# Hymba layer, one core: the MLP's down-projection as seven block products, with its left factors formed in the up-projection, and the first pair of each token half as eight block products

## The chip, the cores and the metric

One core of one Trainium2 chip. The metric is the device time in microseconds (us) of the whole kernel, from a launch on the chip. The kernel before took a median of 3212.68 us in three runs (3212.42 to 3213.5).

Engines: PE is TensorE (matrix products, with weights loaded by PEld), DVE is VectorE, ACT is ScalarE, POOL is GpSimd, SP issues the DMAs of this kernel.

## The reference, cut to what matters

The kernel computes one bidirectional encoder layer on 2048 tokens of width 1024 in float32: attention and a state-space group side by side, an output projection, and a squared-ReLU MLP. The change concerns the last three lines of the layer:

```python
m = rms_norm(h, g_pre_mlp[i]) @ w_mlp_up[i]          # 2048 x 1024 times 1024 x 4096
m = jnp.square(jax.nn.relu(m)) @ w_mlp_down[i]       # 2048 x 4096 times 4096 x 1024
h = h + rms_norm(m, g_post_mlp[i])
```

## The kernel before

**Precision.** Every fp32 factor of a matmul is split in two fp32r parts, h = cast(x) on ACT (line 125) and l = x - h on DVE or POOL (line 126). A product is three matmuls: h·h, h·l, l·h. A matmul is 128x128 by 128x512.

**Order.** The program is written in loops, and a scheduler decides each engine's order of instructions from its own model of their times. On every engine the instructions then run in that order, and an instruction that waits holds back all behind it. DMAs are issued by SP in one such queue.

**Up-projection** (lines 1244 to 1434). It already uses seven block products for eight (Strassen in Winograd's form). The work is cut into 32 pairs: two halves of the tokens (ct, 1024 each), and in each 16 pairs of hidden blocks of 128 columns (NP = 16). For a pair, `up_prep` loads a 1 MB tile of the up weights (`raw`) and forms the seven left factors from its four blocks: a11, a21+a22-a11, a12, a11-a21, a21+a22, a22, a12-a21-a22+a11. I call them f0 to f6. f0, f2 and f5 are plain blocks; f1, f3, f4 and f6 are sums made by POOL in a tile `st` (line 1264: two, one, one and three operations). Each is split into `ah` and `al`. Tiles `raw` and `st` come from the pool `wraw` with two buffers each, `ah` and `al` from `apool` with nine. The seven right factors, B11, T2, B21, T3, T1, T4, B22, are formed from the normed activations once per token half by `t_slice` (lines 1304 to 1321), for each of four slices k of the inner dimension, and stay in SBUF. `up_pair` multiplies, one product after another: 7 x 4 slices x 3 = 84 matmuls; `up_pair_k`, used for pairs 0, 15 and 16, runs over the slices outside, so that it can begin when the first slice is ready. The output sums of Winograd's form are built from PSUM by DVE, and `relu2` (ReLU and square on ACT, lines 1340 and 1341) gives four blocks of the hidden activations per pair, each written to DRAM (`MD`) with 256 KB.

**Down-projection** (lines 1443 to 1543). Plain: eight blocks b of 512 hidden columns, in each block four quarters c of the tokens. For a quarter the left factors (`mraw`, 256 KB each, four of them) are read back and split, for a block the weights (`raw`, four tiles of 512 KB) are loaded and split. `down` does, for each tile of 128 tokens and each half of the outputs, 4 x 3 = 12 matmuls into one PSUM tile (line 1514) and adds it on DVE to the sum `acc` in SBUF (line 1519). So a block and a quarter take 96 matmuls. In the last block `finish` follows each token tile: sum of squares on ACT, gain on DVE, 1/rms on POOL, scale and residual on DVE, output.

Of the kernel before, what the change touches and what calls it, by code (L numbers as in the profile page):

```python
# [51 lines left out]
def hymba_layer_kernel(  # L52
# [53 lines left out]

    HTD = mk(dram, [2, 4, 128, 4, 512], "HTD")
    MD = mk(dram, [2, FF // 128, 128, 1024], "MD")
# [1062 lines left out]
    tst = hw.enter_context(pool("tst", 2))  # L1171
    wraw = hw.enter_context(pool("wraw", 2))
# [17 lines left out]
    def out_tile(t, between):  # L1190
# [12 lines left out]
        V.tensor_copy(s2, p[:, 0:4])  # L1203
# [45 lines left out]
    def up_prep(n):  # L1249
# [6 lines left out]
        for first, *more in ((a11,), (a21, (add, a22), (sub, a11)), (a12,), (a11, (sub, a21)), (a21, (add, a22)),  # L1256
                             (a22,), (a12, (sub, a21), (sub, a22), (add, a11))):
# [23 lines left out]
    for t in range(NT):  # L1281
        last.append((t, out_tile(t, lambda: hn_T(*last.pop(0)) if len(last) == 2 else None)))
        if t in (10, 11):
            s_load(0, t - 10)
        if t >= NT - 7:
            facs.append(next(prep))
# [9 lines left out]
    upr = up_.enter_context(pool("upr", 6, "right"))  # L1296
# [7 lines left out]
    def t_slice(ct, k):  # L1304

        raw = RAW.pop((ct, k))
        b11, b12, b21, b22 = (raw[:, i] for i in range(4))
        l = {n: rt() for n in (T1, T3, T2, T4)}
        split(b11, *TB[B11, k], G)
        G.tensor_tensor(out=l[T1], in0=b12, in1=b11, op=ALU.subtract)  # L1310
        V.tensor_tensor(out=l[T3], in0=b22, in1=b12, op=ALU.subtract)
        V.tensor_tensor(out=l[T2], in0=b22, in1=l[T1], op=ALU.subtract)
        G.tensor_tensor(out=l[T4], in0=l[T2], in1=b21, op=ALU.subtract)
        split(l[T2], *TB[T2, k])
        split(b21, *TB[B21, k])
        split(l[T3], *TB[T3, k])
        split(l[T1], *TB[T1, k])
        split(l[T4], *TB[T4, k])
        split(b22, *TB[B22, k], G)
        if (ct, k + 2) in ((ct, 2), (ct, 3)):  # L1320
            s_load(ct, k + 2)
# [15 lines left out]

    def relu2(c, src, n, odd, half):

        S.activation(out=c, in_=src, func=AF.Relu)  # L1340
        S.activation(out=c, in_=c, func=AF.Square)
        ct, j = n // NP, n % NP
        Y.dma_start(out=MD[ct, 2 * j + odd][:, half * 512:(half + 1) * 512], in_=c)

# [75 lines left out]

    def stepper(n):

        nxt = up_prep(n + 1)

        def step(i):
            facs.append(next(nxt))
        return step

    t_slice(0, 0)
    t_slice(0, 1)  # L1430
    up_pair_k(0, stepper(0), lambda k: t_slice(0, k + 2) if k < 2 else None)
    hn_T(*last.pop(0))
    for n in range(1, NP - 1):
        up_pair(n, stepper(n))
    s_load(1, 0)
    s_load(1, 1)
    up_pair_k(NP - 1, stepper(NP - 1), lambda k: t_slice(1, k))
    up_pair_k(NP, stepper(NP), lambda k: None)
# [5 lines left out]
    FB = 4  # L1444
    NB = FF // 128 // FB
    dps = [ctx.enter_context(pool("dp0", FB))]
    draw = ctx.enter_context(pool("draw", 1))

    def d_load(b):
        for q in range(FB):  # L1450
            fo = (b * FB + q) * 128
            raw = draw.tile([128, D], F32, tag="raw", name="raw")
            Y.dma_start(out=raw, in_=w_mlp_down[0, fo:fo + 128, :])
            dh = dps[b % 2].tile([128, D], F32R, tag="dh", name="dh")
            dl = dps[b % 2].tile([128, D], F32R, tag="dl", name="dl")
            split(raw, dh, dl)
            yield dh, dl

    def m_load(b, c):

        for q in range(FB):
            raw = draw.tile([128, 512], F32, tag="mraw", name="mraw")
# [106 lines left out]
```

## Time and profile before

| what | value |
|---|---|
| median of three runs | 3212.68 us |
| the profiled execution's own time | 3213.55 us |
| its span, first to last instruction | 3211.7 us |
| mean granted TensorE clock | 0.973 |
| PE / DVE / ACT / POOL busy | 94% / 58% / 51% / 39% |
| up-projection's first matmul | 1859.1 us after the span's start |
| last matmul of the down-projection | 3201.9 us |

Busy shares are averages over the whole span; the parts before 1840 us are the attention, the state-space group and the output projection, which the change leaves alone. A row of a group gives busy time, mean length of one in ns, and after the bar the idle time of the engine ahead of them with what ended it. A row of the timeline gives start, length, engine, line and operation, output and inputs, and in brackets the idle time before it and what released it.

### The profile page before, as it was taken

To read this page: it belongs to the slowest core of one execution; us is meant where nothing else is said; L and a number is where in the kernel's file an instruction comes from. 1 tells how busy PE (TensorE), PEld (TensorE's weight loads), DVE (VectorE), ACT (ScalarE), POOL (GpSimd) and SP (SyncE) were. 2 spreads that over 40 slices of the span, in tenths; PEclk is the share of its full clock that TensorE was granted. 3 is DMA by queue.
4 is the path that set the end of the run, shared out by engine and by line. 5 is a ranking of instruction groups with operands and counts; after the bars stand their busy time and mean duration, and the time that the engine had idled before them with its cause. 6 is when DMAs were issued, how large, how long until landed. Compare 5 with 4: busy or idle time off the path is not lost.

```text
span 3211.7 us, 42406 instructions
## 1 busy us (share of the span) xinstructions
PE 3032.7 (94%) x14455; PEld 2419.7 (75%) x14455; DVE 1848.8 (58%) x2893; ACT 1638.6 (51%) x3081; POOL 1255.2 (39%) x2363
## 2 busy tenths in 40 slices
PE   6999988989999999999879879999999999999998
PEld 6899956666777766678767658886888888888887
DVE  6333278767888876675356584448444234444447
ACT  4333356988777799974435445445445421111112
POOL 4222245775888876600032275447544000000002
PEclk8999989999999999999989989999999999999999
DMA  4232231211001022232246543333333422222215
GB/s 151 65 86 74 73 75 27 58 46 33 20 18 27 24 70 85 65 113 63 65 112 179 164 154 115 109 114 119 109 107 106 142 81 73 73 79 73 69 63 203
DMA packets 244377, 279.51 MB, mean 87 GB/s; under 512 B 35920, under 2 KB 180688, under 8 KB 243136
## 3 DMA queue, kind: packets, MB, share of 16 engines
q1 hardware_dynamic: 242112, 275.10, 28.1%
q8 instruction: 113, 1.85, 0.2%
q10 hardware_dynamic: 1792, 1.57, 0.2%
q14 instruction: 104, 0.85, 0.1%
q0 software_dynamic: 256, 0.14, 0.0%
HBM read 181.31 MB, written 95.36 MB: 86 GB/s over the span
## 4 chain that ended last, share of the span: by engine, by line
PE 57%; issue 6%; DVE 4%; ACT 4%; POOL 3%; DMA 2%; SPq 0%; POOLq 0%; DVEq 0%; ACTq 0%
PE dn L1514 20%; PE pE L1329 5%; PE pB L1329 5%; PE pA L1329 4%; PE s L619 3%; PE s L621 2%; PE s L620 2%; PE z L1079 2%; PE X L611 2%; PE pF L1329 2%; PE X L612 2%; PE X L613 2%; PE mxp L573 2%; POOL rs_r L132 1%; DMA rb<-RD 1%
## 5 line engine op out<-in xcount | busy, mean ns | idle before, releaser
L627 DVE TENSOR_TENSOR pl<-s,ph 128x512 fp32r<-128x512 f32 x512 | 350.2, 686 | 163.1 <-ACT s L626 157.0
L623 ACT ACTIVATE ph<-s 128x512 fp32r<-128x512 f32 (+1 forms) x544 | 323.4, 595 | 171.9 <-PE s L621 158.6
L1514 PE MATMUL dn<-dl,ah 128*128 128x512 f32 x1024 | 398.8, 389 | 0.0
L1514 PE MATMUL dn<-dh,ah 128*128 128x512 f32 x1024 | 398.8, 389 | 0.0
L1514 PE MATMUL dn<-dh,al 128*128 128x512 f32 x1024 | 398.7, 390 | 0.0
L574 DVE TENSOR_REDUCE mx<-mxp 128x1 f32<-128x512 f32 x512 | 343.0, 684 | 59.3 <-PE mxp L573 56.2
L125 ACT CAST ah<-mraw 128x512 fp32r<-128x512 f32 x128 | 79.5, 621 | 454.3 <-DMA mraw<-MD 273.8
L626 ACT ACTIVATE s<-s 128x512 f32<-128x512 f32 x512 | 304.1, 594 | 0.7
L1498 POOL TENSOR_TENSOR ss<-s2f 128x1 f32<-128x1 f32 x16 | 11.2, 699 | 702.2 <-ACT jk L1495 702.2
L1264 POOL TENSOR_TENSOR st<-raw 128x512 f32<-128x512 f32 x128 | 173.9, 1359 | 263.6 <-DVE al L126 263.5
L619 PE MATMUL s<-ql,kh 96*128 96x512 f32 (+1 forms) x544 | 226.9, 417 | 15.1 <-ACT ZS L937 4.9
L611 PE MATMUL X<-pl,vt 128*65 128x512 f32 x512 | 209.2, 409 | 29.8 <-DVE pl L627 27.9
L1519 DVE TENSOR_TENSOR acc<-dn,acc 128x512 f32<-128x512 f32 x224 | 153.0, 687 | 133.2 <-PE dn L1514 132.8
L1514 PEld LDWEIGHTS dn<-dl,ah 128*128 128x128 f32 x1024 | 192.4, 188 | 39.8
L1514 PEld LDWEIGHTS dn<-dh,al 128*128 128x128 f32 x1024 | 192.4, 188 | 39.7
L1514 PEld LDWEIGHTS dn<-dh,ah 128*128 128x128 f32 x1024 | 192.3, 188 | 39.7
L620 PE MATMUL s<-qh,kl 96*128 96x512 f32 (+1 forms) x544 | 218.3, 401 | 0.0
L621 PE MATMUL s<-qh,kh 97*128 97x512 f32 (+1 forms) x544 | 215.0, 401 | 0.7 <-DMA qh<-nm 0.7
L573 PE MATMUL mxp<-kh,qh 96*128 96x512 f32 x512 | 199.3, 411 | 13.2 <-DVE mx L574 5.2
L612 PE MATMUL X<-ph,vt 128*64 128x512 f32 x512 | 205.3, 401 | 0.0
L613 PE MATMUL X<-ph,vt 128*65 128x512 f32 x512 | 205.1, 401 | 0.0
L126 DVE TENSOR_TENSOR al<-mraw,ah 128x512 fp32r<-128x512 f32 x128 | 88.5, 691 | 197.8 <-ACT ah L125 188.2
(811 smaller groups left out, 7822.8 us busy)
## 6 DMA issues: line engine op xcount, KB each, us to landing
raw<-in_w_mlp_up_dram SPq DMA_DIRECT2D x32, 1024.0 KB
MD<-r SPq DMA_DIRECT2D x128, 256.0 KB
mraw<-MD SPq DMA_DIRECT2D x128, 256.0 KB
xt<-in_x_dram SPq DMA_DIRECT2D x32, 512.0 KB
raw<-in_w_mlp_down_dram SPq DMA_DIRECT2D x32, 512.0 KB
ug<-UD SPq DMA_DIRECT2D x32, 256.0 KB
HD<-o SPq DMA_DIRECT2D x16, 512.0 KB
traw<-HTD SPq DMA_DIRECT2D x8, 1024.0 KB
```

What stands on the lines that cost most here:

```text
L574: V.reduce_max(out=mxs[n][:, j, b:b + 1], in_=p, axis=AX.X)
L611: T.matmul(out=X[:65], lhsT=v[:, t, 0:65], rhs=pl_, start=(t == 0), stop=False)
L612: T.matmul(out=X[:64], lhsT=v[:, t, 65:129], rhs=ph_, start=False, stop=False)
L613: T.matmul(out=X[:65], lhsT=v[:, t, 0:65], rhs=ph_, start=False, stop=False)
L619: T.matmul(out=s[:m], lhsT=kh[0:96, cs], rhs=ql, start=True, stop=False)
L620: T.matmul(out=s[:m], lhsT=kl[:, cs], rhs=qh[0:96], start=False, stop=False)
L621: T.matmul(out=s[:m], lhsT=kh[:, cs], rhs=qh, start=False, stop=True)
L623: S.activation(out=ph_[:m], in_=s[:m], func=AF.Exp, scale=SCALE)
L626: S.activation(out=s, in_=s, func=AF.Exp, scale=SCALE)
L627: V.tensor_tensor(out=pl_, in0=s, in1=f(ph_), op=ALU.subtract)
L1329: T.matmul(out=p, lhsT=a[:, k], rhs=b, start=(first and k == 0 and j == 0), stop=(k == 3 and j == 2), skip_group_check=not first)
L1514: T.matmul(out=p, lhsT=a[:, ts_], rhs=c[:, hs], start=(q == 0 and w == 0), stop=(q == FB - 1 and w == 2))
```

## The change

**Down-projection.** The product of hidden activations (token halves x hidden blocks) and weights (hidden blocks x output halves) is taken in Winograd's form too. A unit is a block b of 512 hidden columns (two pairs) and a quarter g of the tokens, in which two sets of 128 tokens are paired with two others. It has seven products of 2 token sets x 2 inner blocks x 3 = 12 matmuls: 84. The left factors (a11, a12, a21, a22, s1 = a21+a22, s2 = s1-a11, s4 = a12-s2, a11-a21) are formed in `relu2` of the up-projection, two on DVE and two on POOL; `MD` keeps seven blocks for each pair, so seven writes of 256 KB instead of four, and the down-projection reads seven tiles per unit. The right factors are formed from the weights by `w_factors`: per block 14 POOL operations (lines 1555), 14 casts and 14 subtractions, spread over the last unit (g = 3) of the block before, into a ring of 16 buffers. The seven results go into `acc` with DVE operations from PSUM (12 per unit) and POOL operations in SBUF (6 per unit, lines 1652, 1661, 1662).

**First pairs.** Pair 0 and pair 16 use eight block products (`up_pair_c`, 96 matmuls): they need only the plain blocks B11, T4's place used for b12, B21 and B22. The T slices are formed later: T1 to T3 from the raw tiles (slices 0 and 1 on POOL), T4 afterwards on POOL from the split parts.

**Buffers.** `wraw` has one buffer instead of two, so one `raw` and one `st`; `tst` 3 instead of 2, `upr` 8 instead of 6. `finish` splits the scaling over DVE, ACT and POOL and takes its two work tiles from the pool `wr` of two buffers.

```diff
-    MD = mk(dram, [2, FF // 128, 128, 1024], "MD")
+    MD = mk(dram, [2, FF // 256, 128, 7, 512], "MD")
...
-    tst = hw.enter_context(pool("tst", 2))
-    wraw = hw.enter_context(pool("wraw", 2))
+    tst = hw.enter_context(pool("tst", 3))
+    wraw = hw.enter_context(pool("wraw", 1))
...
+        for first, *more in ((a11,), (a12,), (a21,), (a22,)) if j == 0 else seven:
...
+    def b_slice(ct, k):
+        raw = RAW[ct, k]
+        for i, n in enumerate((B11, T4, B21, B22)):
+            split(raw[:, i], *TB[n, k])
...
+    def t_slice(ct, k, eng=V):
         raw = RAW.pop((ct, k))
...
+        eng.tensor_tensor(out=t1, in0=b12, in1=b11, op=ALU.subtract)
+        eng.tensor_tensor(out=t3, in0=b22, in1=b12, op=ALU.subtract)
+        eng.tensor_tensor(out=t2, in0=b22, in1=t1, op=ALU.subtract)
...
+        for n, t in ((T2, t2), (T3, t3), (T1, t1)):
+            split(t, *TB[n, k])
+    def t4_slice(k):
+        (th, tl), (bh, bl) = TB[T2, k], TB[B21, k]
+        t = rt()
+        G.tensor_tensor(out=t, in0=f(th), in1=f(tl), op=ALU.add)
+        G.tensor_tensor(out=t, in0=t, in1=f(bh), op=ALU.subtract)
+        G.tensor_tensor(out=t, in0=t, in1=f(bl), op=ALU.subtract)
+        split(t, *TB[T4, k])
...
     def relu2(c, src, n, odd, half):
         S.activation(out=c, in_=src, func=AF.Relu)
         S.activation(out=c, in_=c, func=AF.Square)
...
+        if len(blocks) == 4:
+            a11, a12, a21, a22 = (blocks.pop(x) for x in ((0, 0), (1, 0), (0, 1), (1, 1)))
+            s1, s2, s4 = rt(), rt(), rt()
+            V.tensor_tensor(out=s1, in0=a21, in1=a22, op=ALU.add)
+            put(4, s1)
+            V.tensor_tensor(out=a21, in0=a11, in1=a21, op=ALU.subtract)
+            put(3, a21)
+            G.tensor_tensor(out=s2, in0=s1, in1=a11, op=ALU.subtract)
+            put(1, s2)
+            G.tensor_tensor(out=s4, in0=a12, in1=s2, op=ALU.subtract)
+            put(6, s4)
...
+    def w_factors(b):
...
+        for first, *more in ((b11,), (b22, (sub, b12), (add, b11)), (b21,), (b22, (sub, b12)), (b12, (sub, b11)),
+                             (b22, (sub, b12), (add, b11), (sub, b21)), (b22,)):
+            for fp in range(2):
...
+                    for op, x in more:
+                        G.tensor_tensor(out=st, in0=src, in1=blk(x), op=op)
+                        src = st
+                split(src, h, l)
...
+    def down(b, g, step):
...
+        for i in range(7):
...
+                for fp in range(2):
...
+                    for j, (x, y) in enumerate(((mh, wh), (mh, wl), (ml, wh))):
+                        T.matmul(out=ps, lhsT=x[:, c], rhs=y, start=(first and fp == 0 and j == 0),
+                                 stop=(fp == 1 and j == 2), skip_group_check=not first)
...
+                if i == 0:
+                    S.copy(out=p1, in_=ps)
+                elif i == 1:
+                    V.tensor_tensor(out=u2, in0=ps, in1=p1, op=ALU.add)
+                    if b > 0:
+                        G.tensor_tensor(out=c12, in0=c12, in1=u2, op=ALU.add)
...
+                elif i == 3:
+                    V.tensor_tensor(out=u3, in0=ps, in1=p1, op=ALU.add)
+                    if b > 0:
+                        G.tensor_tensor(out=c22, in0=c22, in1=u3, op=ALU.add)
+                        G.tensor_tensor(out=c21, in0=c21, in1=u3, op=ALU.add)
```

What this makes of the order shows at three places. The first is POOL in the up-projection, before the change; `st<-raw` opens a factor, `st<-st,raw` continues it, and the numbers tell the tiles apart (raw_22420 and raw_22574 belong to two pairs).

```order
L1264 TENSOR_TENSOR st_22548<-raw_22420 128x512
L1264 TENSOR_TENSOR st_22548<-st_22548,raw_22420 128x512
L1264 TENSOR_TENSOR st_22595<-raw_22574 128x512
L1264 TENSOR_TENSOR st_22548<-st_22548,raw_22420 128x512
L1264 TENSOR_TENSOR st_22595<-st_22595,raw_22574 128x512
L1264 TENSOR_TENSOR st_22635<-raw_22574 128x512
L1264 TENSOR_TENSOR st_22658<-raw_22574 128x512
L1264 TENSOR_TENSOR st_22702<-raw_22574 128x512
```

The next pair's f1 stands among the operations of f6. The same place after the change, where L1371 is s2 and L1373 is s4 of the pair whose products run:

```order
L1371 TENSOR_TENSOR r_23099<-r_23098,r_23011 128x512
L1266 TENSOR_TENSOR st_23034<-raw_22973 128x512
L1373 TENSOR_TENSOR r_23100<-r_23073,r_23099 128x512
L1266 TENSOR_TENSOR st_23057<-raw_22973 128x512
L1266 TENSOR_TENSOR st_23111<-raw_22973 128x512
L1266 TENSOR_TENSOR st_23111<-st_23111,raw_22973 128x512 x2
L1266 TENSOR_TENSOR st_23158<-raw_23137 128x512
L1266 TENSOR_TENSOR st_23158<-st_23158,raw_23137 128x512
L1266 TENSOR_TENSOR st_23198<-raw_23137 128x512
L1371 TENSOR_TENSOR r_23263<-r_23262,r_23175 128x512
L1373 TENSOR_TENSOR r_23264<-r_23237,r_23263 128x512
L1266 TENSOR_TENSOR st_23221<-raw_23137 128x512
```

The next pair's f1 now stands behind all of f6; f3 stands between s2 and s4 in one pair and ahead of s2 in the next, and f4 and f6 always behind s4. The second place is SP in the same stretch, after the change: the weight load of a pair among the writes of `MD`.

```order
L1359 DMA MD_81<-r_23098 128x512
L1359 DMA MD_81<-r_23099 128x512
L1359 DMA MD_81<-r_23094 128x512
L1359 DMA MD_81<-r_23100 128x512
L1359 DMA MD_81<-r_23175 128x512
L1254 DMA raw_23137<-in_w_mlp_up_dram 128x8x256
L1359 DMA MD_81<-r_23214 128x512
```

r_23098 to r_23100 are s1, s2, a11-a21 and s4 of one pair, r_23175 is the first block of the next. Before the change the load stood behind a pair's first block in the same way, with no sums in front. The third place is DVE in the down-projection after the change, in a unit g = 3: `al` are left factors, `wl` right factors of the next block, the other rows take results from PSUM.

```order
L127 TENSOR_TENSOR wl_28020<-wst_28021,wh_28019 128x512
L1668 TENSOR_TENSOR acc_26685<-pE_27892,acc_26685 128x512
L127 TENSOR_TENSOR al_28043<-mraw_28040,ah_28042 128x512
L1650 TENSOR_TENSOR u2_27949<-pB_27988,p1_27948 128x512
L1650 TENSOR_TENSOR u2_27952<-pB_27997,p1_27951 128x512
L127 TENSOR_TENSOR wl_28047<-raw_27976,wh_28046 128x512
L127 TENSOR_TENSOR al_28075<-mraw_28072,ah_28074 128x512
L127 TENSOR_TENSOR wl_28051<-raw_27978,wh_28050 128x512
L1657 TENSOR_TENSOR acc_26685<-pA_27954,acc_26685 128x512
L1657 TENSOR_TENSOR acc_26685<-pA_27962,acc_26685 128x512
L127 TENSOR_TENSOR wl_28079<-wst_28080,wh_28078 128x512
L127 TENSOR_TENSOR al_28109<-mraw_28106,ah_28108 128x512
```

Before the change DVE's rows there are additions into `acc` from PSUM and an `al` or `dl` after every second of them; now operations on two SBUF inputs and evictions alternate.

More of the change, by code (lines that the diff above doesn't have):

```diff
@@ L1419, in up_pair_k, with up_pair_c, step, before @@
         slices(3)
+    def up_pair_c(n, before, behind, step):
+        mine = take()
+        outs = []
+        for half, (b1, b2) in enumerate(((B11, B21), (T4, B22))):
+            for odd in range(2):
+                outs.append((pa("c"), odd, half, mine[2 * odd], mine[2 * odd + 1], b1, b2))
+        for k in range(4):
+            before(k)
+            for i, (p, odd, half, a1, a2, b1, b2) in enumerate(outs):
+                for w, (left, b) in enumerate(((a1, b1), (a2, b2))):
+                    ah, al = left
+                    bh, bl = TB[b, k]
+                    for j, (x, y) in enumerate(((ah, bh), (ah, bl), (al, bh))):
+                        T.matmul(out=p, lhsT=x[:, k], rhs=y, start=(k == 0 and w == 0 and j == 0),
+                                 stop=(k == 3 and w == 1 and j == 2))
+                if k == 3:
+                    relu2(rt(), p, n, odd, half)
+                    if i > 0:
+                        step()
+            if k in (1, 2):
+                step()
+            if k == 2:
+                step()
+            behind(k)
+        step()
     def stepper(n):
         nxt = up_prep(n + 1)
-        def step(i):
-            facs.append(next(nxt))
-        return step
[L1429 to L1432, printed above, removed]
+        def step(i=None):
+            w = next(nxt, None)
+            if w is not None:
+                facs.append(w)
+        return step
+    b_slice(0, 0)
+    b_slice(0, 1)
+    t_slice(0, 0, G)
+    b_slice(0, 2)
+    def before(k):
+        if k == 1:
+            hn_T(*last.pop(0))
+            t_slice(0, 1, G)
+        elif k == 2:
+            b_slice(0, 3)
+            t_slice(0, 2)
+        elif k == 3:
+            t_slice(0, 3)
+    up_pair_c(0, before, t4_slice, stepper(0))
     for n in range(1, NP - 1):
         up_pair(n, stepper(n))
[L1435 to L1438, printed above, removed]
+    for k in range(3):
+        s_load(1, k)
+    def behind(k):
+        b_slice(1, k)
+        t_slice(1, k)
+    up_pair_k(NP - 1, stepper(NP - 1), behind)
+    up_pair_c(NP, lambda k: None, t4_slice, stepper(NP))
     for n in range(NP + 1, 2 * NP - 1):
@@ L1441, in hymba_layer_kernel @@
     hw.close()
[L1444 to L1457, printed above, removed]
@@ L1459, in m_load @@
-    def m_load(b, c):
-        for q in range(FB):
-            raw = draw.tile([128, 512], F32, tag="mraw", name="mraw")
-            Y.dma_start(out=raw, in_=MD[c // 2, b * FB + q][:, (c % 2) * 512:(c % 2) * 512 + 512])
-            mh = apool.tile([128, 4, 128], F32R, tag="ah", name="ah").rearrange("p k c -> p (k c)")
-            ml = apool.tile([128, 4, 128], F32R, tag="al", name="al").rearrange("p k c -> p (k c)")
-            split(raw, mh, ml)
-            yield mh, ml
-    ds, ms = [], []
@@ L1499, in finish @@
         r = rstd_of(st, D)
[L1500 removed]
+        for half, eng in ((0, V), (1, G)):
             hs = slice(half * 512, (half + 1) * 512)
[L1502 to L1519 removed]
@@ new lines, in hymba_layer_kernel, with step @@
+    parts = [(b, g) for b in range(NB) for g in range(4)]
+    for _ in nm:
+        pass
+    for n, (b, g) in enumerate(parts):
+        nm = m_factors(*parts[n + 1]) if n + 1 < len(parts) else iter(())
+        if g == 3:
+            nwf = w_factors(b + 1) if b + 1 < NB else iter(())
+        def step(i, behind):
+            if behind:
+                next(nm, None)
+                if g == 3:
+                    next(nwf, None)
+                    next(nwf, None)
+            elif n == 0:
+                while len(WF) <= i:
+                    next(nwf, None)
+        down(b, g, step)
+        if g == 3:
+            for _ in nwf:
+                pass
+            del WF[:7]
```

181 lines of the change are left out of this document (112 added, 69 removed).

## The prediction

> **What bounds the kernel now.** I read the page's busy times first, then the chain of waits, then the table by stretches for the two stages that the change rewrites.
>
> ```profile
> PE 3032.7 (94%) x14455; PEld 2419.7 (75%) x14455; DVE 1848.8 (58%) x2893; ACT 1638.6 (51%) x3081; POOL 1255.2 (39%) x2363
> 2508.86 625.62 PE dn L1514 x2761
> L1514 PE MATMUL dn<-dl,ah 128*128 128x512 f32 x1024 | 398.8, 389 | 0.0
> 2260.00:2320.00 60.00, 60.00 (x266) 49.71 (x266) 26.48 (x38) 28.62 (x50) 28.15 (x22) 1.00 0.35 115
> 2600.00:2700.00 100.00, 100.00 (x442) 82.85 (x442) 44.35 (x63) 17.87 (x25) 0.00 (x0) 1.00 0.25 82
> ```
>
> Columns of the stretches: length, then PE, PEld, DVE, ACT, POOL busy with counts, granted clock, DMA share, GB/s. TensorE alone sets the end of both stages: it is busy 60.00 of 60 us in the up-projection and 100.00 of 100 in the down-projection, at clock 1.00, and its 3 x 1024 down matmuls have no idle ahead of them. 100 us hold 442 matmuls: 0.2262 us from start to start. In the down-projection DVE has 56 us of 100 free, POOL all 100. The change spends that slack on fewer matmuls; whether the helpers still hide is the question.
>
> **Matmuls removed.** A down unit (block b of 512 hidden columns, quarter g of the tokens) takes 7 products x 2 x 2 x 3 = 84 matmuls where 96 stood; 32 units save 384 x 0.2262 = **-86.9**. The two first pairs get 12 more each, 2.7 us apiece, counted below.
>
> **The start of the up-projection.**
>
> ```profile
> 1859.13 0.80 PE L1329 MATMUL p<-T00h,ah 128*128 128x512 f32 x1 [7.12 <-ACT T00h L125]
> 1860.00:1880.00 20.00, 11.44 (x32) 7.75 (x32) 19.91 (x16) 7.99 (x15) 17.17 (x11) 0.74 0.33 104
> 1880.00:1895.00 15.00, 11.58 (x35) 7.88 (x36) 15.00 (x12) 5.98 (x11) 13.77 (x9) 0.77 0.26 87
> L1378 DVE TENSOR_TENSOR r<-pE,u x4: 684/691/692, 2172.2 to 2281.6; 128x512 f32<-128x512 f32 x4
> 1863.00 1.75 DVE L1312 TENSOR_TENSOR r<-traw,r 128x512 f32<-128x512 f32 x1
> 1864.16 1.74 POOL L126 TENSOR_TENSOR T60l<-traw,T60h 128x512 fp32r<-128x512 f32 x1
> ```
>
> The eviction L1378 closes pairs 14, 17, 18 and 19. From the first matmul to pair 14's close at 2172.2 are 313 us; fifteen pairs of 84 matmuls are 285, so 28 us are lost, 20 of them in the 35 us from 1860 to 1895, where DVE has no free moment and TensorE does 67 matmuls (15 us). After the change pair 0 needs only sixteen splits of raw blocks, so its 96 matmuls (21.7 us) run beside the forming of the T slices. If DVE still ends that at about 1898, 39 us after the first matmul, 17 are lost, 14 if pair 1 begins 3 us early on the first slices: a gain of 14, less 2.7 for the twelve matmuls: **-11**. DVE has about ten more operations over the four slices. Bounds: 0 if ten at 1.1 us (between 0.69 and 1.75) come on top, -20 if the slices keep up with pair 1.
>
> **The change of token half.** From pair 14's close to pair 19's, 2172.2 to 2281.6 in the row above, are 109.4 us for five pairs, where 5 x 84 x 0.2262 = 95.0, so 14 us are lost now. A slice goes from seven DVE operations to eleven, four slices from 28 to 44; sixteen times 0.69 is 11 us, half of it behind pair 16's matmuls that need no T. I take +5 and 2.7 for the twelve matmuls: **+8** (0 to +18).
>
> **The factor loop of the up-projection**, the largest cost. Now two weight buffers and two `st` tiles let POOL start the next pair's factors before the last are done; the change keeps one of each, and puts s2 and s4 between the factor operations.
>
> ```profile
> L1264 POOL TENSOR_TENSOR st<-raw 128x512 f32<-128x512 f32 x26 | 33.5, 1290 | 66.8 <-DVE al L126 66.8
> L126 DVE TENSOR_TENSOR al<-st,ah 128x512 fp32r<-128x512 f32 x26 | 22.1, 852 | 23.4 <-ACT ah L125 23.3
> L126 DVE TENSOR_TENSOR al<-raw,ah 128x512 fp32r<-128x512 f32 x19 | 13.0, 686 | 0.4
> 2300.60 0.69 DVE L1378 TENSOR_TENSOR r<-pE,u 128x512 f32<-128x512 f32 x1 [2.91 <-PE pE L1329]
> 2302.37 0.63 ACT L1341 ACTIVATE r<-r 128x512 f32<-128x512 f32 x1
> 2304.50 0.62 ACT L125 CAST ah<-st 128x512 fp32r<-128x512 f32 x1 [1.51 <-PE pA L1329]
> 2304.69 1.29 POOL L1264 TENSOR_TENSOR st<-st,raw 128x512 f32<-128x512 f32 x1
> 2305.16 1.37 DVE L126 TENSOR_TENSOR al<-st,ah 128x512 fp32r<-128x512 f32 x1 [1.91 <-ACT ah L125]
> 2306.61 1.29 POOL L1264 TENSOR_TENSOR st<-raw 128x512 f32<-128x512 f32 x1 [0.62 <-DVE al L126]
> 2307.86 2.54 POOL L1264 TENSOR_TENSOR st<-st,raw 128x512 f32<-128x512 f32 x2
> 2311.24 0.38 SPq L1253 DMA_DIRECT2D raw<-in_w_mlp_up_dram  x1
> 2330.29 0.38 SPq L1253 DMA_DIRECT2D raw<-in_w_mlp_up_dram  x1
> GB/s 0 0 12 94 109 240 335 385 388 399 334 46 0 0 0 0 0 12 0 215 173 0 0 21 361 6 0 0 0 0 0 70 117 243 308 360 385 414 343 76
> ```
>
> Take the last eviction of a pair (2300.60) as zero. Its square ends at +2.4 (2302.37 + 0.63); the new s1 on DVE (0.69) ends at +3.1; s2 and s4 on POOL (1.29 each) end at +5.7. Before f4 may overwrite `st`, f3 must have been cast and subtracted: 0.62 + 0.69 and handoffs, about 1.35 from POOL's end to POOL's next start. In the changed order every other pair has f3 ahead of s2, the others between s2 and s4. In the first kind f4 runs +5.7 to +7.0, f6 (three operations) +8.35 to +12.2. The single weight buffer is then free, the 1 MB load is issued 0.6 later (2306.61 to 2310.40 is f6 now, the issue 2311.24), and its bytes land 4.9 to 5.7 us later (the GB/s row has 40 slices of 2310 to 2337: 1 MB from 2311.24 is there by about 2317, shared with two writes, from 2330.29 by about 2335.2). So +17.7 to +18.5, a cast after 0.45 and 0.62 more: the next pair's first factor at +18.8 to +19.6, needed at +18.7 (19.04 from pair to pair, the eviction 0.3 after the last matmul). In the second kind f3 takes 1.37 more in the same queue: +20.1 to +20.9. The mean lateness of the two kinds is (0.5 + 1.8)/2, about 1.2 us a pair; for 28 pairs **+34**. No TensorE work is put in between pairs to cover it. Bounds: 0 if landing and handoffs are 1 us shorter; 2.6 a pair, +73, if POOL's six operations of the loop each take 1.72 as in the head instead of 1.29. I take the low side since the 26 and 18 POOL operations of this stretch held 1.29 while DVE ran; it is DVE that waits (852 for 686 ns).
>
> **Up to down, and the first block of right factors.** f3, f4 and f5 of the first block wait on POOL behind the last pair's s2 and s4: 14 operations x 1.29 = 18 us against 19 of one unit, begun late by about 5.7. TensorE's order takes the next unit's first products ahead; I take 4.5 there and 2 at the first change of block: **+6.5** (0 to +15).
>
> **Right factors in the later blocks.**
>
> ```profile
> L1519 DVE TENSOR_TENSOR acc<-dn,acc 128x512 f32<-128x512 f32 x224 | 153.0, 687 | 133.2 <-PE dn L1514 132.8
> ```
>
> In units g = 1, 2 DVE has 19 operations (13 us of 19.0) and POOL six (7.7): hidden. Around a change of block POOL has 14 + 12 operations in two units, 33.5 us of 38.1; DVE has 53, of which 24 read PSUM at 0.69 as in the row, and 29 read SBUF twice at 0.69 to 1.37. That is 36.6 us if none meets a POOL operation and 56 if all do. With half of POOL's 26 operations delaying one by 0.68, 45.4; the next unit's spare 6 us cannot be borrowed wholly, because f5's products are due in the unit before. I take 4 for each of six changes: **+24** (0 to +48).
>
> **The end.**
>
> ```profile
> 3201.85 0.39 PE L1514 MATMUL dn<-dh,al 128*128 128x512 f32 x1
> 3203.26 1.28 DVE L1519 TENSOR_TENSOR acc<-dn,acc 128x512 f32<-128x512 f32 x2
> 3207.08 1.41 DVE L1502 SCALAR_TENSOR_TENSOR jk<-acc,rs_r,ht 128x512 f32<-128x512 f32 x2 [0.99 <-POOL rs_r L132]
> 3202.71 6.15 SPq L1503 DMA_DIRECT2D out_dram<-jk  x4
> ```
>
> One token tile is finished behind the last matmul now, 9.9 us to the span's end at 3211.7. Afterwards four are, in two buffers: the second two load their residual only when the first two have been written. That is another round of square, sum, scale and write (3203.26 to 3208.5 and a transfer), less what overlaps: **+8** (+4 to +14).
>
> **Sum.** -86.9 - 11 + 8 + 34 + 6.5 + 24 + 8 = -17.4. The profiled execution took 3213.55 us, 0.87 above the runs' median of 3212.68: 3213.55 - 17.4 - 0.87 = **3195**.
>
> **Rivals.**
> *A, the helpers hide.* The scheduler's order lets the factor loop fit 19.0 us and DVE's overlaps fall on TensorE's own pace: terms 34 and 24 go. 3195 - 58 = 3137. For it: DVE and POOL are under half busy in the up-projection now. Against: the loop above has no slack even at 1.29.
> *B, DVE and POOL take turns (slower).* Where both always have a next operation with two SBUF inputs, the head shows 1.75 beside 1.74 instead of 0.69 beside 1.29. If that holds in the loop, 2.6 a pair (+73), and 8 at each change of block (+48): 3195 + 39 + 24 = 3258. It decides once the loop costs over 1.2 + 17.4/28 = 1.8 us a pair, all else as forecast. For it: nine POOL and two more DVE operations a pair, no second buffer to run ahead. Against: POOL holds 1.29 in the stretch at 2260. The Trainium skill's page "Trainium Architecture — The Big Picture", section "What this means for kernel authors", calls the port that VectorE and GpSimd share an exclusive lock, not a split of bandwidth; by that rule two full queues add their durations, 0.69 + 1.29 = 1.98 by the rows, and the head's 1.75 comes near it, while in the up-projection only the later one waits (1.37).
> *C, no net change.* The change of half loses 18 instead of 8 and the start gains nothing, by the extra splits on DVE: 3195 + 10 + 11 = 3216.
>
> **How the numbers follow.** The forecast 0.42, with its own range 3165 to 3220; A 0.24; B 0.30; C 0.04. Differences under 0.2% (6.4 us) can hardly be told from none. Of the forecast 0.30 lies over 0.2% below the time before, 0.07 within, 0.05 above; A is all faster, B all slower, C within or above by halves. Faster 0.54, same 0.09, slower 0.37. The range 3130 to 3272 takes in A, and B but for the loop's and the blocks' upper bounds together.
>
> **What would show it.** Pair to pair, the eviction that closes a pair should come every 20.2 us instead of 19.0, with TensorE waiting for ACT's cast `ah<-raw` of a pair's first factor, and that cast for the weight load; at 19.0 A holds, at 21.6 B. POOL's `st` operations should stay at 1.29 (B: 1.7). Plain units should come every 19.0 us, the two around a change of block 42. In the 39 us after the up-projection's first matmul TensorE should do over 100 matmuls, and 18 us should lie behind the last matmul of all. The forecast is wrong if TensorE waits for something unnamed here: the read of left factors in 1 KB rows, say, or s4's wait in front of the weight load in SP's queue.

## The result: 3358.72 us, 4.5% slower

The changed kernel takes a median of 3358.72 us (3356.41 to 3362.8, four runs), the kernel before beside it 3213.09 us (3212.42 to 3217.21): a ratio of 1.045, 95% interval 1.043 to 1.047. I had forecast 3195 us, in a range of 3130 to 3272. The sign is that of rival B, the size lies outside the range. The page of the profile after, busy times and the chain by engine:

```profile
PE 3039.4 (90%) x14095; PEld 2376.0 (71%) x14095; DVE 2258.6 (67%) x3259; ACT 1763.1 (52%) x3329; POOL 1813.4 (54%) x2707
PE 9%; DVE 8%; POOL 7%; DMA 5%; issue 3%; ACT 2%; DVEq 0%; ACTq 0%; POOLq 0%
```

TensorE ran 360 matmuls fewer and had 57% of that chain before; now it has 9%, and DVE, POOL and DMA stand beside it. The table by stretches of the kernel after (length, PE, PEld, DVE, ACT, POOL busy with counts, granted clock, DMA share, GB/s) covers the up-projection's two halves with the change between them, the first block of the down-projection, the six middle blocks and their lead into the last, the last block, the end:

```profile
1855.50:2200.00 344.50, 300.29 (x1199) 232.19 (x1200) 211.51 (x222) 143.37 (x248) 204.10 (x138) 0.94 0.39 128
2200.00:2276.00 76.00, 63.07 (x241) 48.42 (x241) 57.75 (x72) 38.04 (x68) 41.63 (x25) 0.89 0.41 142
2276.00:2636.00 360.00, 321.78 (x1283) 250.11 (x1281) 206.57 (x222) 145.01 (x251) 215.56 (x146) 0.93 0.37 123
2636.00:2736.00 100.00, 86.52 (x358) 69.48 (x357) 74.91 (x99) 44.49 (x79) 37.86 (x26) 0.93 0.43 131
2736.00:3235.00 499.00, 475.33 (x2032) 379.42 (x2031) 435.99 (x542) 175.66 (x301) 346.96 (x226) 0.99 0.38 114
3235.00:3331.00 96.00, 78.74 (x304) 59.98 (x302) 87.27 (x103) 39.31 (x87) 73.58 (x74) 0.91 0.52 167
```

No stretch is full any more, where 60.00 of 60 and 100.00 of 100 us stood before. The stages of the two profiled executions, in us. A pair is taken to begin with the fourth matmul of its first product (`pA<-T01h,ah`), since the first three are sometimes drawn into the pair before:

| stage | before | after | difference | forecast |
|---|---|---|---|---|
| first up matmul, from the span's start | 1859.1 | 1855.5 | -3.6 | 0 |
| to pair 1's first product | 40.0 | 26.5 | -13.5 | -11 |
| pair 1 to pair 14 | 247.7 | 318.1 | +70.4 | about +16 |
| pair 14 to pair 17, the change of half | 71.8 | 76.1 | +4.3 | +8 and 3.6 |
| pair 17 to the up-projection's last matmul | 289.8 | 359.8 | +70.0 | about +15 |
| down-projection to its last matmul | 693.4 | 694.2 | +0.8 | -56.4 |
| last matmul to the span's end | 9.8 | 30.8 | +21.0 | +8 |

The start of a stage 1860 us into the kernel differed by up to 14 us between the kernels of this study (1847.8 to 1862.2), so the first row is not counted as an effect of the change. Three losses remain: 140 us in the up-projection, a down-projection that gave back all of its 86.9 us, and 21 us at the end.

**The factor loop.** Selected rows of two pairs of the kernel after, engines mixed by time (start, length, engine, line and operation, and in brackets the idle time with what ended it). L1409 closes a pair; `st<-raw` opens a factor and `st<-st,raw` continues it. First a pair with f3 ahead of s2:

```profile
2404.80 0.62 ACT L126 CAST ah<-raw 128x512 fp32r<-128x512 f32 x1 [1.28 <-DMA raw<-in_w_mlp_up_dram]
2406.66 0.68 DVE L1409 TENSOR_TENSOR r<-pE,u 128x512 f32<-128x512 f32 x1
2409.34 1.67 POOL L1266 TENSOR_TENSOR st<-raw 128x512 f32<-128x512 f32 x1 [1.46 <-DVE al L127]
2411.64 1.79 POOL L1371 TENSOR_TENSOR r<-r 128x512 f32<-128x512 f32 x1 [0.63 <-DVE r L1367]
```

Then the next one, with f3 between s2 and s4:

```profile
2422.27 0.38 SPq L1254 DMA_DIRECT2D raw<-in_w_mlp_up_dram  x1
2426.32 0.69 DVE L1409 TENSOR_TENSOR r<-pE,u 128x512 f32<-128x512 f32 x1 [2.10 <-PE pE L1341]
2428.57 0.62 ACT L126 CAST ah<-raw 128x512 fp32r<-128x512 f32 x1 [3.02 <-DMA raw<-in_w_mlp_up_dram]
2428.68 1.27 POOL L1266 TENSOR_TENSOR st<-raw 128x512 f32<-128x512 f32 x1 [6.44 <-DMA raw<-in_w_mlp_up_dram]
2429.22 1.28 DVE L127 TENSOR_TENSOR al<-raw,ah 128x512 fp32r<-128x512 f32 x1 [2.21 <-ACT ah L126]
2430.03 1.60 POOL L1266 TENSOR_TENSOR st<-st,raw 128x512 f32<-128x512 f32 x1
2430.42 1.76 DVE L1367 TENSOR_TENSOR r<-r 128x512 f32<-128x512 f32 x1
2432.26 1.29 POOL L1371 TENSOR_TENSOR r<-r 128x512 f32<-128x512 f32 x1 [0.63 <-DVE r L1367]
2434.19 1.67 POOL L1266 TENSOR_TENSOR st<-raw 128x512 f32<-128x512 f32 x1 [0.63 <-DVE al L127]
2435.82 1.74 POOL L1373 TENSOR_TENSOR r<-r 128x512 f32<-128x512 f32 x1
2438.19 1.29 POOL L1266 TENSOR_TENSOR st<-raw 128x512 f32<-128x512 f32 x1 [0.63 <-DVE al L127]
2440.93 1.67 POOL L1266 TENSOR_TENSOR st<-raw 128x512 f32<-128x512 f32 x1 [1.46 <-DVE al L127]
2442.69 2.65 POOL L1266 TENSOR_TENSOR st<-st,raw 128x512 f32<-128x512 f32 x2
2445.36 0.38 SPq L1254 DMA_DIRECT2D raw<-in_w_mlp_up_dram  x1
```

From weight load to weight load are 23.09 us: 6.3 until the first cast has the data, then f1, s2, f3, s4, f4 and f6 one after the other on POOL, nine operations of 13.2 us together with 3.5 of waits between them, and the next load. Over the ten loads from 2340 to 2600 us the means are 5.9, 13.3 and 3.9. The pair before had closed at 2426.32, but f1 of the next pair stands ahead of s2 in POOL's order and waits for the load. So s2 and s4 run behind the landing. In DVE's order s1 (L1367) stands behind the next pair's first split in the same way; by the bracket at L1371 this holds POOL for only 0.63 us.

**The end.** Last matmul, the loads of residuals, the squares they release and the last writes of the kernel after:

```profile
3330.17 0.45 PE L1642 MATMUL pE<-wh,al 128*128 128x512 f32 x1
3337.42 1.63 SPq L1600 DMA_DIRECT2D fin<-HD  x2
3337.45 0.63 ACT L1604 ACTIVATE fin<-acc 128x512 f32<-128x512 f32 x1 [5.37 <-DMA out_dram<-fin]
3348.29 1.00 SPq L1600 DMA_DIRECT2D fin<-HD  x2
3348.32 0.63 ACT L1604 ACTIVATE fin<-acc 128x512 f32<-128x512 f32 x1 [5.55 <-DMA out_dram<-fin]
```

Until 3337 two token tiles of the unit before are finished, then come two rounds of two tiles each, 11 us to the next load and 12.7 to the end. By the brackets the squares shown waited for a write to be out.

### The profile page after: what moved, and what is told of

It reads as the page before. It is cut to its first block, busy times and chain, and to the rows that moved or that the text cites. A ratio compares the mean times of both kernels' runs of the same rounds, so it can differ in the third digit from the quotient of the medians.

```text
span 3361.0 us, 43408 instructions
## 1 busy us (share of the span) xinstructions
PE 3039.4 (90%) x14095; PEld 2376.0 (71%) x14095; DVE 2258.6 (67%) x3259; ACT 1763.1 (52%) x3329; POOL 1813.4 (54%) x2707
## 5 line engine op out<-in xcount | busy, mean ns | idle before, releaser
L1266 POOL TENSOR_TENSOR st<-raw 128x512 f32<-128x512 f32 x120 | 182.7, 1523 | 259.6 <-DMA raw<-in_w_mlp_up_dram 166.7
L126 ACT CAST ah<-mraw 128x512 fp32r<-128x512 f32 x224 | 138.5, 621 | 289.9 <-DMA mraw<-MD 241.1
L127 DVE TENSOR_TENSOR al<-mraw,ah 128x512 fp32r<-128x512 f32 x224 | 235.3, 1052 | 54.9 <-ACT ah L126 50.6
L620 PE MATMUL s<-ql,kh 96*128 96x512 f32 (+1 forms) x544 | 226.3, 416 | 13.2 <-ACT ZS L938 4.9
L127 DVE TENSOR_TENSOR al<-st,ah 128x512 fp32r<-128x512 f32 x120 | 127.6, 1064 | 127.7 <-ACT ah L126 123.9
L574 PE MATMUL mxp<-kh,qh 96*128 96x512 f32 x512 | 200.3, 413 | 12.8 <-DVE mx L575 5.1
L132 POOL TENSOR_SCALAR rs_v<-ss 128x1 f32<-128x1 f32 (+1 forms) x98 | 20.5, 209 | 350.8 <-ACT kvn L325 119.0
L126 ACT CAST ah<-st 128x512 fp32r<-128x512 f32 x120 | 74.4, 620 | 208.4 <-POOL st L1266 208.2
L1555 POOL TENSOR_TENSOR wst<-raw 128x512 f32<-128x512 f32 x64 | 97.5, 1529 | 103.0 <-DVE wl L127 91.8
L127 DVE TENSOR_TENSOR al<-raw,ah 128x512 fp32r<-128x512 f32 x98 | 105.9, 1083 | 65.7 <-ACT ah L126 65.7
L620 PEld LDWEIGHTS s<-ql,kh 96*128 96x128 f32 (+1 forms) x544 | 103.5, 190 | 60.2 <-ACT ZS L938 7.1
L574 PEld LDWEIGHTS mxp<-kh,qh 96*128 96x128 f32 x512 | 100.2, 197 | 51.3 <-DVE mx L575 8.1
```

The lines of the kernel that those rows point to most:

```text
L126: S.copy(out=h, in_=src)
L127: eng.tensor_tensor(out=l, in0=src, in1=f(h), op=ALU.subtract)
L574: T.matmul(out=p, lhsT=qs[n][0][0:96, j * 128:(j + 1) * 128], rhs=kh[0:96, b * 512:(b + 1) * 512])
L620: T.matmul(out=s[:m], lhsT=kh[0:96, cs], rhs=ql, start=True, stop=False)
L1266: G.tensor_tensor(out=st, in0=src, in1=b, op=op)
```

## The experiments

Theory LOOP: the single weight buffer puts load and POOL's work one behind the other, and that sets the pair. Rival PORT: the collisions of DVE and POOL operations set it, whatever the buffers.

### Two weight buffers

```diff
-    tst = hw.enter_context(pool("tst", 3))
+    tst = hw.enter_context(pool("tst", 2))
     wraw = hw.enter_context(pool("wraw", 1))
+    wrawr = hw.enter_context(pool("wrawr", 2))
...
-        raw = wraw.tile([128, 8, 256], F32, tag="raw", name="raw")
+        raw = wrawr.tile([128, 8, 256], F32, tag="raw", name="raw")
```

The third slice buffer goes back to two, and the slice loads in `t_slice` move with it.

> The changed kernel with two buffers for the up weights' tile raw (st stays single); room for it from tst, 2 instead of 3. Theory LOOP: with one raw buffer the load, f1, s2, f3, s4, f4 and f6 stand one behind the other, 23.05 us a pair; with two the load leaves this chain and a pair takes 19.0 to 19.4. 13 + 14 pairs and three in the change of half gain about 3.9 each: about -115, 3240 to 3250 us. Rival PORT: operations of DVE and POOL that get in each other's way set the pair's time, whatever the buffers: pairs stay at 22 or more, 3330 or more.

Measured: 3242.33 us, 1.0088 of before (1.0071 to 1.0105), 116 us less than the change. From pair 1 to 14 are 274.6 us instead of 318.1; the last pairs of each half come every 19.04 us, as fast as TensorE works. LOOP stands. The longest of TensorE's waits in the up-projection (total, times, longest), first with two buffers and then in the change:

```profile
PE pE L1342 <- DVE r L1400: 10.0, 8, 3.1
```
```profile
PE pA L1341 <- ACT ah L126: 45.2, 23, 3.3
PE pA L1341 <- DVE al L127: 12.3, 22, 0.6
```

The wait for a pair's first factor (pA, 45.2 us in 23 waits) is gone from the head of the list. The operations themselves stay long; here are POOL's and DVE's from 2100 to 2176 us of the kernel with two buffers, while its pairs come every 19.04 us:

```profile
L1267 POOL TENSOR_TENSOR st<-raw 128x512 f32<-128x512 f32 x15 | 21.2, 1410 | 12.7 <-DVE al L127 12.7
L127 DVE TENSOR_TENSOR al<-raw,ah 128x512 fp32r<-128x512 f32 x13 | 16.7, 1281 | 0.0
```

Not all of the 140 us is the buffer's: against the kernel before, 27 us remain between pairs 1 and 14 and 23 behind pair 17.

### The kernel before with single buffers

```diff
-    wraw = hw.enter_context(pool("wraw", 2))
+    wraw = hw.enter_context(pool("wraw", 1))
```

> The kernel before with the pool wraw at one buffer instead of two, nothing else changed. LOOP: the chain is then load 6.3, f1 2.6, f3 1.3, f4 1.3, f6 3.9 and three handoffs of about 1.4: 19.6 to 20.2 a pair instead of 19.04, so +15 to +35 us: 3230 to 3248; small, since s2 and s4 are not in it. PORT: no operation was added, so no change: 3210 to 3216.

Measured: 3275.34 us, 1.0195 of before (1.0179 to 1.021): +62. The weight loads mostly come every 20.5 to 20.8 us, 1.6 over TensorE's 19.04, where I had expected 0.6 to 1.2. Between pairs 1 and 14 this costs 22 us, behind pair 17 another 17; the change of half takes 90.5 instead of 71.8, and the down-projection 704.7 instead of 693.4, which is not explained. PORT falls as the rival of the buffer. But POOL's operations, though none was added, are longer here too: 1.40 to 1.48 us on average where the kernel before has 1.31 to 1.35. LOOP holds, at a higher price than mine, above all where slices and factors share the queues.

### s2 and s4 on DVE

```diff
-            G.tensor_tensor(out=s2, in0=s1, in1=a11, op=ALU.subtract)
+            V.tensor_tensor(out=s2, in0=s1, in1=a11, op=ALU.subtract)
             put(1, s2)
-            G.tensor_tensor(out=s4, in0=a12, in1=s2, op=ALU.subtract)
+            V.tensor_tensor(out=s4, in0=a12, in1=s2, op=ALU.subtract)
```

> The changed kernel with one raw buffer as it is, s2 and s4 formed on DVE instead of POOL. LOOP: two POOL operations of about 1.6 and their waits leave the chain: 23.05 becomes 19.5 to 20.5 a pair, -75 to -100 us: 3260 to 3285. PORT: DVE has two more operations with two SBUF inputs, POOL two fewer, the same collisions: within 20 us of 3359.

Measured: 3311.55 us, 1.0306 of before (1.0291 to 1.0322), 47 less than the change; loads mostly every 21.4 to 21.6 us. That lies between the two forecasts and fits neither. The two operations leave POOL, 10.1 us a pair where it had 13.3, but stand then in DVE's queue ahead of splits that POOL's next operation waits for: POOL's waits between its operations grow from 3.9 to 5.7 us a pair.

### Two weight buffers and finish in place

```diff
-        both = wr.tile([128, 2, 1024], F32, tag="raw", name="fin")
-        ht, jk = both[:, 0], both[:, 1]
+        i = fins[0] % 2
+        if i == 0:
+            fins[1] = wr.tile([128, 2, 1024], F32, tag="raw", name="fin")
+        fins[0] += 1
+        ht = fins[1][:, i]
         Y.dma_start(out=ht, in_=HD[t])
+        jk = acc[:, t]
...
-            S.activation(out=jk[:, hs], in_=acc[:, t, hs], func=AF.Square, accum_out=ss[:, half:half + 1])
+            dump = wst.tile([128, 512], F32, tag="st", name="dump")
+            S.activation(out=dump, in_=acc[:, t, hs], func=AF.Square, accum_out=ss[:, half:half + 1])
```

> As e1, and finish works in place: the scaled result is written over acc and sent from there, the two wr tiles hold the residuals of four token tiles, squares go to a dump tile. If the end is long because the third and fourth tile wait until the first two have been written out, 30.8 us behind the last matmul become 12 to 15 and the last block loses about 10 of its 19: 25 to 30 us less than e1, about 3215. If the DMAs themselves are the bound, the end stays over 25 us and the gain under 8.

Measured: 3230.62 us (1.0056 of before, 1.0041 to 1.0071), 11.7 less than with two buffers alone. That is less than half of what I expected. The end shrinks from 31.1 to 16.0 us, close to the 12 to 15 expected, but the down-projection ahead of it grows by 7.0: the last block, from its first `pF` matmul to the last matmul of all, takes 96.3 us instead of 88.8. I read this as finishing work that had waited and now meets the evictions; no run separates it.

### No right factors in later blocks

```diff
-            nwf = w_factors(b + 1) if b + 1 < NB else iter(())
+            nwf = iter(())
...
-            del WF[:7]
+            pass
```

> As the run with two weight buffers and the in-place finish (3230.6 us), but the right factors of block 0 are used in all eight blocks: the loads of the down weights, 14 POOL sums, 14 casts and 14 subtractions per later block are left out, so the output is not that of the layer. Theory CHANGE OF BLOCK: these are what lengthens the two units around a change (+5 to +6 us for each of six, and +9 before the last block): the first units of blocks then come every 76.2 us, 38 to 48 us less, 3183 to 3193. Rival: the reading and splitting of left factors beside POOL's additions into acc is enough to hold DVE back; then blocks stay at 79 or more and the gain is under 20.

Measured: 3186.74 us, 44 less. I time a block from the first `pF` matmul of its first unit to that of the next block's. With the factors these are 78.4, 79.9, 81.8, 81.9, 85.1, 82.0 and 81.4 us; without, 78.6 and then 76.2 six times, which is 4 x 84 matmuls with nothing lost. So plain units hide all their work, and a change of block costs 5.3 us on average, 2 to 9 each (4 forecast).

### What of the right factors it is

Three runs ask for the share of DVE's and POOL's part: fewer sums by building them on one another, then in later blocks no low parts, or no sums. The first as a diff:

```diff
+        for i, first in enumerate((b11, b22, b21, None, b12, None, b22)):
...
+                if i == 1:
+                    G.tensor_tensor(out=keep[3, fp], in0=src, in1=blk(b12), op=sub)
+                    G.tensor_tensor(out=keep[1, fp], in0=keep[3, fp], in1=blk(b11), op=add)
+                    src = keep[1, fp]
+                elif i == 3:
+                    src = keep[3, fp]
...
+                elif i == 5:
+                    src = keep[1, fp]
+                    G.tensor_tensor(out=src, in0=src, in1=blk(b21), op=sub)
```

> As the run with two weight buffers and the in-place finish, and the sums of the right factors are built on one another (b22-b12, plus b11, minus b21): 8 POOL operations per block instead of 14, at the price of four st tiles held longer, upr at 6, and the gain vector loaded in the last block. COLLISION: DVE's splits are late because POOL's sums hold the port; six fewer of POOL's 26 operations around a change of block save 2 to 3 us of each change and 3 in the first block: 3205 to 3220. DVE COUNT: DVE's 53 operations in two units set the delay by themselves: within 5 us of 3230.

Measured: 3223.60 us (1.0035 of before, 1.0022 to 1.0048), 7 less. The first block gains 5.5 us (19.7 from the up-projection's last matmul to the first `pF` instead of 25.2) and the last block 9.1 (87.2 for 96.3); the end loses 5.3. The later blocks still take 77.8 to 83.8 us, 2.5 less in all. That spoke for DVE's count. The second and third:

```diff
-                split(src, h, l)
-                both.append((h, l))
+                if b == 0:
+                    split(src, h, l)
+                else:
+                    S.copy(out=h, in_=src)
+                both.append((h, l or h))
```

> As the run with two weight buffers and the in-place finish (3230.6 us, blocks every 78.4 to 85.1 us), but in blocks 1 to 7 the 14 subtractions that form the low parts of the right factors are left out and the high part stands in their place in the matmuls, so the output is not that of the layer. The 14 POOL sums, casts and loads stay. DVE COUNT: 39 DVE operations instead of 53 around a change of block fit easily, and blocks fall to 76.2 to 77.5: about 3192. POOL QUEUE: the additions into acc that DVE's evictions wait for stand behind the factor sums in POOL's queue; then blocks stay at 80 or more, over 3215.

```diff
-                if more:
+                if more and b == 0:
```

> The same base, but in blocks 1 to 7 the 14 POOL sums are left out and the plain blocks are cast and split in their place (output not that of the layer); DVE keeps all 53 operations. POOL QUEUE or COLLISION: with 12 POOL operations instead of 26 blocks fall to 76.2 to 77.5, about 3192. DVE COUNT: 80 or more stay, over 3215.

Measured: 3196.74 us without the low parts (blocks 76.2 to 76.7 from the second interval on), 3201.63 without the sums (76.2 to 79.6, mean 77.6), one time each, without an interval. Either cure works, though the blocks without the sums do not quite come down to 76.2. So neither DVE COUNT nor POOL QUEUE alone is right: the loss needs DVE's 53 operations and POOL's 26 together. DVE's splits of left factors over 480 us of the middle blocks (2600 to 3080), first with both, then without the low parts, then without the sums:

```profile
L127 DVE TENSOR_TENSOR al<-mraw,ah 128x512 fp32r<-128x512 f32 x163 | 177.2, 1089 | 32.2 <-ACT ah L126 31.1 <-PE pF L1650 0.8
```
```profile
L127 DVE TENSOR_TENSOR al<-mraw,ah 128x512 fp32r<-128x512 f32 x175 | 183.2, 1051 | 52.3 <-ACT ah L126 51.4 <-PE pF L1653 0.4
```
```profile
L127 DVE TENSOR_TENSOR al<-mraw,ah 128x512 fp32r<-128x512 f32 x172 | 150.7, 880 | 37.8 <-ACT ah L126 37.1
```

With the sums the split takes 1089 ns on average, without them 880; the low parts add 14 splits of the right factors around each change. Either alone nearly fits two units, both do not. In the down-projection before, the same split took 691 ns, with POOL idle.

### All sums built on one another, with one and with two weight buffers

The left factors likewise: f4 = a21+a22, f1 = f4-a11, f6 = a12-f1, four POOL operations per pair instead of seven, in three `st` tiles; with the in-place finish, the right factors' shorter sums and six `r` tiles instead of eight.

```diff
+                    G.tensor_tensor(out=kept[4], in0=src, in1=more[0][1], op=add)
+                    G.tensor_tensor(out=kept[1], in0=kept[4], in1=more[1][1], op=sub)
...
+                elif more[0][1] is None:
+                    G.tensor_tensor(out=kept[1], in0=src, in1=kept[1], op=sub)
```

> One weight buffer as in the change; in-place finish; sums built on one another in the right factors as in the run beside it and in the left factors too (f4 = a21+a22, f1 = f4-a11, f6 = a12-f1: four POOL operations per pair instead of seven, with three st tiles). LOOP: three POOL operations of about 1.6 and one handoff of 1.45 leave the chain of 23.05 us: 16.8 to 18.5, so TensorE's 19.04 binds and this run comes within 15 us of the same kernel with two weight buffers. PORT: the collisions between s2, s4 and the splits remain, pairs stay over 21, 55 us or more above it.

> The same with two weight buffers, a candidate for the fastest: 4 POOL operations per pair instead of 7 also shorten the stalls of the up-projection after the change of token half, where the run with seven still lost about 25 us: 10 to 15 us below the run with reused down sums alone, 3192 to 3208. If those stalls come from DVE alone, no difference between the two.

Measured: 3229.72 us with one buffer (1.0051 of before, 1.0036 to 1.0066), 3195.13 us with two (0.9941, 0.9925 to 0.9958), the fastest kernel of the study that still computes the layer, and 0.6% faster than the kernel before. With one buffer the loads mostly come every 19.5 to 20.4 us: even with four sums the chain stays over 19.04, against my 16.8 to 18.5. It runs another way there. From 2300 to 2500 us s2 on POOL waits 30.1 us for s1 in ten waits, and ACT's ReLU waits 20.7 us for s2 in nine; a cast of the plain block f5 stands behind that ReLU, and the load goes out when f5 is split. Whether the six `r` tiles cause this was not tested. This run is 35 us above the one with two buffers, so both forecasts (within 15, 55 or more) missed. From pair 1 to pair 14 the two-buffer kernel takes 265.5 us, 9.0 less than with seven sums, and 271.8 instead of 282.1 from pair 17 to 31. In its last block 26 us over the plain pace remain, and 20.3 behind it.

### First pairs undone

The kernel of 3195.13 us with `up_pair_k`, `t_slice` and the order of slices of the kernel before in pairs 0, 15 and 16.

```diff
-    up_pair_c(0, before, t4_slice, stepper(0))
+    up_pair_k(0, stepper(0), lambda k: t_slice(0, k + 2) if k < 2 else None)
...
-    up_pair_k(NP - 1, stepper(NP - 1), behind)
-    up_pair_c(NP, lambda k: None, t4_slice, stepper(NP))
+    up_pair_k(NP - 1, stepper(NP - 1), lambda k: t_slice(1, k))
+    up_pair_k(NP, stepper(NP), lambda k: None)
```

> The fastest kernel so far (3195 us: two weight buffers, in-place finish, sums built on one another) with the first pairs of both token halves as before the change: seven products, T slices formed first. From the first up matmul to pair 14 that kernel takes 290.4 us (before: 287.8) and from 14 to 17 62.6 us (before: 71.8). If the eight block products are worth what I estimated at the start (11 us) and cost 8 at the change of half, this run is 3 us slower; by the measured stages the change of half gains 9, and undoing it costs 9 to 20: 3204 to 3215.

Measured: 3207.63 us (0.9983 of before, 0.9973 to 0.9992), 12.5 more. First up matmul to pair 17: 360.8 us with the old first pairs, 352.9 with the new: 7.9 us, namely 10.4 at the change of half (73.0 against 62.6) and 2.5 the other way before pair 14. The two profiled executions differ by 8.2 us in all, so the stages account for these and not for all of the 12.5 between the medians. Before pair 14 the new first pair gains 15.8 us to pair 1's first product (24.9 against 40.7), but from pair 1 to pair 14 it loses 18.3 (265.5 against 247.2, and 247.7 in the kernel before). The head start is given back in the pairs behind it.

### Less of finish on DVE

```diff
-            V.tensor_tensor(out=jk[:, hs], in0=jk[:, hs], in1=ht[:, hs], op=ALU.add)
+            eng.tensor_tensor(out=jk[:, hs], in0=jk[:, hs], in1=ht[:, hs], op=ALU.add)
```

> The 3195 us kernel with the residual of the second output half added by POOL instead of DVE in finish: two DVE and two POOL operations per token tile and not three and one. If DVE's load is what lengthens the last block (its units take 18 to 31 us, 14 more than 76 in all), 4 to 10 us less: about 3188. If POOL's turn on the shared operands costs as much, no difference or slower.

Measured: 3202.5 us (0.9969 of before, 0.9956 to 0.9982), 7.4 more than without the edit. Down-projection and end together take 698.6 us against 697.8: the first gains 9.7, the end loses 10.5. Moving the work to POOL changes where it waits, not how long. Of the 5.2 us between the two profiled executions 4.7 lie ahead of the first up matmul, which this edit does not touch.

## Why the prediction was wrong

**Matmuls removed (-86.9): right.** Blocks of 76.2 us, 4 x 84 matmuls, appear wherever the helper engines keep up.

**The start (-11): right to pair 1's first product and no further.** There it is -13.5, with 116 matmuls in the 39 us where I had asked for over 100. But the run with the first pairs undone shows that the 15.8 us that the new first pair gains there are followed by 18.3 lost up to pair 14: a loss that my sum did not have, hidden in the kernel after under the loop's. **The change of half (+8)**: +4.3 with the loop's own 4 us a pair inside it, -9.2 with two weight buffers (62.6 against 71.8). The sign was wrong: undoing the new pair costs 10.4.

**The factor loop (+34, measured 140): the step that failed.** I counted from a pair's close and put six POOL operations between it and the next load (s2, s4, f4 and three for f6), as if the next pair's f1, and in one kind of pair its f3, were done by then. The load was to go out 12.8 us after the close, or 14.2 in the other kind. In the two pairs shown it goes out 15.6 and 19.0 after it (2406.66 to 2422.27, 2426.32 to 2445.36). f1 cannot start before its weights have landed, and it stands ahead of s2 in POOL's order. So all nine POOL operations of a pair lie between one landing and the next load, and the loop closes over the load, not over the pair's close: 23.05 us, not 20.2. For 27 pairs that is 108 us; the rest is in the first pairs of each half, where slices and factors share DVE and POOL. The order's POOL rows could have told it: I had read the place of f3 there, and not that of f1.

The second fault is a size. I took POOL's operations at 1.29 us; nine took 13.3 us where nine at 1.29 are 11.6. That is, as an estimate, 1.7 of the 2.9 us by which my 20.2 was too short. My price of the load was right: over ten loads its first consumer came 5.6 to 6.3 us behind it, 5.9 on average, where I had 5.4 to 6.1. The place of s1 behind DVE's first split is a small part, 0.6 to 0.7 us a pair by POOL's waits for it; no run moved s1 forward. The groups of the kernel after, from 2340 to 2600 us:

```profile
L1266 POOL TENSOR_TENSOR st<-raw 128x512 f32<-128x512 f32 x46 | 67.9, 1477 | 99.4 <-DMA raw<-in_w_mlp_up_dram 65.5 <-DVE al L127 33.9
L1266 POOL TENSOR_TENSOR st<-st,raw 128x512 f32<-128x512 f32 x33 | 46.0, 1395 | 2.6
L1373 POOL TENSOR_TENSOR r<-r 128x512 f32<-128x512 f32 x12 | 20.1, 1678 | 0.5
L1371 POOL TENSOR_TENSOR r<-r 128x512 f32<-128x512 f32 x12 | 18.5, 1539 | 7.6 <-DVE r L1367 7.6
L127 DVE TENSOR_TENSOR al<-st,ah 128x512 fp32r<-128x512 f32 x46 | 50.1, 1089 | 51.8 <-ACT ah L126 50.2
L127 DVE TENSOR_TENSOR al<-raw,ah 128x512 fp32r<-128x512 f32 x34 | 36.4, 1071 | 25.7 <-ACT ah L126 25.7
```

**Rival B: half right.** I gave it 3258 and the sign was its own. Its mechanism is there, al 1089 and 1071 ns for 852 and 686, POOL 1395 to 1678 for 1290, and by the estimate above it is 1.7 of the 4.0 us a pair. But alone it did not set the pair: with two buffers the long operations stay and the last pairs of each half return to 19.04, and with one buffer nine operations at 1.29 would still leave the loop at about 21.4. What decided was the single buffer with nine POOL operations behind its load; B named the missing buffer, but priced only the collisions. On my point of decision, 1.8 us a pair, the loop came to 4.0.

**Up to down and first block (+6.5): too low**, 30.7 us from the last up matmul to the first `pF` where five products take 13.6, so +17. The first two rows are TensorE's long waits there; the other two come mostly from later blocks:

```profile
PE pB L1642 <- ACT wh L126: 7.3, 1, 7.3
PE pF L1642 <- ACT wh L126: 5.4, 1, 5.4
PE pE L1642 <- DVE acc L1664: 22.1, 21, 4.7
PE pB L1642 <- DVE u L1650: 11.5, 12, 2.0
```

The 5.4 us are for POOL's sums, as I had it. The 7.3 us are not: the cast of a sum that had been formed since 2300 us stood in ACT's order behind a cast that waited for a left factor to be read back.

```profile
2645.26 0.62 ACT L126 CAST ah<-mraw 128x512 fp32r<-128x512 f32 x1 [2.65 <-DMA mraw<-MD]
2645.79 1.13 ACT L126 CAST wh<-wst 128x512 fp32r<-128x512 f32 x2
```

I had named the reading of left factors as something that would make the forecast wrong, and had not priced it.

**Right factors in later blocks (+24, measured 41): right mechanism, size too small.** The seven intervals of the change add up to 574.4 us, 41 over 7 x 76.2; 5.9 each where I had 4.

**The last block (not priced, measured +26.5)** is a term that I left out: from its first `pF` to the last matmul are 89.1 us for 62.5 of matmuls. `finish` of three units runs beside the evictions there; I had priced it at the end only. From 3241 to 3331 us TensorE waits 11.2 us for evictions of one kind (L1664) alone, and DVE does 31 operations of `finish`; no run takes `finish` out, so its share is argued. At the end the **+8 was 21**: I had counted one more round of finishing and there are two, each waiting for a write; with room for four tiles the end is 16.0 us and not 31.

**Rivals A and C** fall: of what A needs only the plain units came out, and C's price for the change of half has the wrong sign.

## What to carry to other kernels

When one buffer of a double buffer is given up, write down the chain from load to load in every engine's order, the in-order queue of each engine that the chain crosses included; an operation of the last round that stands behind a wait for the next load joins the chain. Count from load to load, not from the end of a product. A slack of 50% on two helper engines is not 50% if both read two SBUF operands: here DVE's splits went from 0.69 to 1.1 us and POOL's operations from 1.29 to 1.5, on average. A head start has to be followed to the stage's end: here 15.8 us at the start were 2.5 lost by pair 14. Work that is moved off a full engine has to be counted at the busiest unit (here a change of block, the last block), not over the stage.

## What the runs showed of the hardware that I had not expected

The granted clock was lower where TensorE often waited for a short time: 0.94 and 0.93 in the up-projection's halves after the change, 0.91 in the last block, against 0.97, 1.00 and 1.00 in the same stages before. Matmuls that follow a wait of 1 to 5 us take 0.49 to 0.80 us instead of 0.39. In the up-projection the loop sets the pace anyway; in the down-projection's first and last block I can't say how much of the loss is the clock, since no run separates it.

POOL's operations were lengthened too, to 1.4 to 1.7 us on average, not only DVE's. In the stretch of the kernel before from which I took 1.29 only DVE's were longer (852 for 686 ns). Why the one or the other gives way was not tested.
